# Experts' second product: 256 row gathers and strip matmuls in place of a dense product with gates

## The chip, the cores and the metric

The kernel runs on one core of a Trainium2 chip. Its time is the device time of one launch in microseconds (us). Three runs of the kernel before gave 1656.79, 1662.8 and 1663.07 us; the median is 1662.8. The core has five instruction queues that matter here: TensorE (PE, with the weight loads shown apart as PEld), VectorE (DVE), ScalarE (ACT), GpSimd (POOL) and SyncE (SP), which issues the loads. Sixteen DMA engines move the data.

## The reference, cut to what matters

The program is three residual layers with their feed-forwards and mixers on 256 tokens of 1,024 channels in float32, and at the end a layer of 16,384 experts, `peer`. Only that last layer is touched.

```python
def peer(h, w_query, sub_keys1, sub_keys2, expert_u, expert_v):     # T = 256 tokens, D = 1024
    q = (hf @ w_query).reshape(T, PEER_HEADS, 2, PEER_QDIM // 2)    # 8 heads
    s1 = jnp.einsum('thc,hkc->thk', q[:, :, 0], sub_keys1)          # 128 first keys
    s2 = jnp.einsum('thc,hkc->thk', q[:, :, 1], sub_keys2)          # 128 second keys
    v1, i1 = lax.top_k(s1, PEER_TOPK)                               # 16 of each
    v2, i2 = lax.top_k(s2, PEER_TOPK)
    cand = (v1[..., :, None] + v2[..., None, :]).reshape(T, PEER_HEADS, PEER_TOPK * PEER_TOPK)
    vc, ic = lax.top_k(cand, PEER_TOPK)
    idx = (e1 * N_KEYS + e2).reshape(T, PEER_HEADS * PEER_TOPK)     # 128 experts per token
    gate = jax.nn.softmax(vc, axis=-1).reshape(T, PEER_HEADS * PEER_TOPK)
    def block(args):                                                # per 128 tokens
        u = expert_u[ib]
        pre = jnp.einsum('td,tkd->tk', xb, u)
        a = jax.nn.gelu(pre, approximate=False) * gb
        return jnp.einsum('tk,tkd->td', a, expert_v[ib])            # the second product
    ...
```

Every token picks 128 of the 16,384 experts. Expert tables `expert_u` and `expert_v` hold 16,384 rows of 1,024 floats each, 64 MB a table.

## The kernel before

The layers ahead of the experts are the same in both kernels and end near 790 us of the span. What follows runs in three stages.

**Queries and scores.** Sixteen steps `q_step` and `s_step`: a unit of 128 x 1,024 weights comes in on SP's queue, ScalarE rounds it to a high part (`whi`, L70), VectorE takes the rest as a low part (`wlo`, L73), and TensorE multiplies high by high, low by high and high by low (`mm_ws`, L351): 24 matmuls of 256 columns. The picks are found by VectorE (`top16`: maxima, their places, their removal) in a background list `bg` from which `run_bg` hands out as much as a step's allowance permits. GpSimd adds the candidates and masks the places; it also makes `dg_p`, from which TensorE spreads the norm's token factors (`rows_of`, L342).

**Up-products.** 128 steps `u_step`, one for each first key `e`: the 128 experts (e, 0..127) against all 256 tokens, 24 matmuls, so the first product is dense: it is made for all experts, picked or not. The result of the Gelu goes to `GS[e // 64][:, e % 64]`, a store of 128 second keys x 128 first keys x 256 tokens. Before them the tokens are normalised in place (`norm_a`, `norm_b`, `norm_c`).

**Gates.** The routing weights are put onto the stored activations by one-hot products (`gate_a`, `gate_mm` L1741, `gate_mul`): 32 steps for each half of `GS`, each of eight tokens and 24 small bfloat16 matmuls. The first half's steps are spread over the last fifty `u_step`s, the second half's over the first sixty steps of the next stage.

**Second product.** 128 units of `expert_v` come in on SP's queue in order, are split in two parts as the weights are, and twelve matmuls of 512 columns a unit (`mm_xs`, L356 to L358) add onto four banks `acc`: dense again, with zero weight for experts that were not picked. At the end the residual `xd` is added and stored.

The order on TensorE, VectorE and ScalarE is that of the program text (`manual_schedule`); SP and GpSimd take their work as the scheduler puts it. `ahead` starts the load and the split of the next unit one step before it is used; four raw buffers and three of each part form the ring.

Of the kernel before, what the change touches and what calls it, by code (L numbers as in the profile page):

```python
# [46 lines left out]
NW = 232  # L47
# [9 lines left out]
def tile_kernel(ctx: ExitStack, tc: tile.TileContext, x, w, eu, ev, pp, cst, rows, ifb, wif, bias, wqk, subk, out, stage=99, dbg=None):  # L57
# [120 lines left out]
    def rsqrt(y, v, n, nm, pool=wk, e=G):  # L178
        """y = v ** -0.5 on [128, n]: the exponent halved through the bits, three Newton steps."""
# [152 lines left out]
    def rows_of(r, at=None, e=G):  # L332
        """r [128, 2] as rows [128, 256], the same on every partition"""
# [12 lines left out]
    def mm_ws(p, hi, lo, off, kn, rh, rl, stride=128):  # L346
        """p[128, n] = sum_k W[:, k]^T x[:, k]: weights stationary"""
# [6 lines left out]
    def mm_xs(p, xhi, xlo, hi, lo, first, last):  # L354
        """p += x^T W (x stationary), three parts"""
# [4 lines left out]
    def xs_block(n=512, tag="mm", hook=None, ps=None, es=()):  # L360
        """one block of n columns, x stationary: two banks [128 tok, n]; the first two units may be done"""
# [38 lines left out]
    # =====================================================================  # L400
    # layer 0: sliding-window attention with sinks beside the S5 mixer
    # =====================================================================
    def even_layer(_):
# [1627 lines left out]
```

## Time and profile before

| | us |
|---|---|
| median of three runs | 1662.8 |
| lowest and highest run | 1656.79, 1663.07 |
| profiled execution, span from the first to the last instruction | 1656.3 |
| TensorE busy in the span | 1616.3 (98%) |
| VectorE, ScalarE, GpSimd busy | 1182.5, 811.5, 196.0 |
| up-products with half of the gate steps | 840.4 to 1254.3 |
| second product with the other half | 1254.3 to 1652.5 |
| mean of the DMA engines | 162 GB/s |

The page lists no time of the profiled execution other than its span; of the three runs the lowest is 0.5 us above it and the median 6.5. A busy TensorE is not one at its peak, since ends of matmuls are modelled; a matmul in float32 shows as two records where its operands are not of the reduced kind.

### The profile page before, as it was taken

The page shows a single profiled execution, that of the slowest core. Times are in us where ns is not written, and L with a number is a line of the kernel's source. Part 1 is how long each engine was busy: PE and PEld are TensorE (multiplying, and loading weights), DVE is VectorE, ACT ScalarE, POOL GpSimd, SP SyncE. Part 2 cuts the span into 40 slices and gives each one's busy share as a digit, 9 for nine tenths or more (in the row PEclk, how much of TensorE's full clock was granted, in tenths as well). Part 3 has the DMA queues.
Part 4 walks back from the last instruction along what each step waited for, and adds up shares of the span by engine and source line. Part 5 has one row for each costly group of instructions (what it writes and reads, how often), then busy time and mean ns, then how long its engine had stood idle before and what let it go on. Part 6 is the DMA issues. An engine that isn't in the chain of part 4 may idle for free.

```text
span 1656.3 us, 29543 instructions
## 1 busy us (share of the span) xinstructions
PE 1616.3 (98%) x11722; PEld 1460.5 (88%) x11722; DVE 1182.5 (71%) x2138; ACT 811.5 (49%) x1367; POOL 196.0 (12%) x345
## 2 busy tenths in 40 slices
PE   5899999999999999999999999999999999999999
PEld 4769999989899998777999999999998888888887
DVE  8787766655666667756799898677777888865555
ACT  4447444557754445476654545433334333344453
POOL 6931100011100000401110324000000000000000
PEclk9969999999999999999999999999999999999999
DMA  5415655553445565534555556544444444456664
GB/s 175 112 38 172 215 186 184 186 173 115 141 153 185 184 190 168 185 112 142 186 171 190 173 189 196 174 136 130 138 132 149 152 150 144 144 180 196 193 191 165
DMA packets 77970, 268.93 MB, mean 162 GB/s; under 512 B 9856, under 2 KB 13060, under 8 KB 77576
## 3 DMA queue, kind: packets, MB, share of 16 engines
q1 hardware_dynamic: 76776, 266.27, 50.4%
q8 instruction: 91, 1.49, 0.4%
q10 hardware_dynamic: 1056, 0.79, 0.2%
q14 instruction: 47, 0.39, 0.1%
HBM read 264.40 MB, written 2.62 MB: 161 GB/s over the span
## 4 chain that ended last, share of the span: by engine, by line
PE 89%; DVE 5%; POOL 3%; ACT 1%; issue 1%; DMA 1%; SPq 0%; POOLq 0%; ACTq 0%; DVEq 0%
PE mm L351 40%; PE acc L356 11%; PE acc L357 11%; PE acc L358 11%; PE mm L1741 3%; PE acc L1741 3%; DVE wlo L73 1%; PE acc L235 1%; POOL cmG L73 1%; PE acc L690 1%; PE mm L766 1%; PE mm L356 1%; PE mm L358 1%; PE mm L357 1%; PE mm L193 0%
## 5 line engine op out<-in xcount | busy, mean ns | idle before, releaser
L73 DVE TENSOR_TENSOR wlo<-raw,whi 128x1024 fp32r<-128x1024 f32 x473 | 588.6, 1246 | 280.9 <-ACT whi L70 271.7
L70 ACT ACTIVATE whi<-raw 128x1024 fp32r<-128x1024 f32 x475 | 502.3, 1058 | 439.2 <-PE acc L357 235.2
L351 PE MATMUL mm<-xh,whi 128*128 128x256 f32 x1472 | 212.3, 287 | 0.0
L351 PE MATMUL mm<-xh,wlo 128*128 128x256 f32 x1472 | 206.8, 283 | 0.0
L351 PE MATMUL mm<-xl,whi 128*128 128x256 f32 x1472 | 206.4, 283 | 0.0
L356 PE MATMUL acc<-whi,vh 128*128 128x512 f32 x512 | 202.1, 395 | 0.0
L357 PE MATMUL acc<-whi,vl 128*128 128x512 f32 x512 | 199.5, 390 | 0.0
L358 PE MATMUL acc<-wlo,vh 128*128 128x512 f32 x512 | 199.3, 389 | 0.0
L351 PEld LDWEIGHTS mm<-xh,whi 128*128 128x128 f32 x1472 | 193.0, 192 | 4.4
L351 PEld LDWEIGHTS mm<-xl,whi 128*128 128x128 f32 x1472 | 189.9, 192 | 0.0
L351 PEld LDWEIGHTS mm<-xh,wlo 128*128 128x128 f32 x1472 | 189.7, 192 | 0.0
L67 ACT ACTIVATE gs<-mm 128x256 f32<-128x256 f32 x128 | 49.2, 385 | 235.5 <-PE mm L351 235.4
L358 PEld LDWEIGHTS acc<-wlo,vh 128*128 128x128 f32 x512 | 96.1, 188 | 20.3
L356 PEld LDWEIGHTS acc<-whi,vh 128*128 128x128 f32 x512 | 96.8, 189 | 19.0
L357 PEld LDWEIGHTS acc<-whi,vl 128*128 128x128 f32 x512 | 96.2, 188 | 19.0
L1741 PEld LDWEIGHTS <-gb 128*128 128x128 bf16 x1536 | 93.5, 118 | 9.3 <-issue 7.8
L73 DVE TENSOR_TENSOR ga<-ga,pkT 128x512 bf16<-128x512 bf16 x192 | 75.4, 421 | 2.2
L351 PE MATMUL mm<-nh,wlo 128*128 128x256 f32 x512 | 70.8, 280 | 0.1
L351 PE MATMUL mm<-nh,whi 128*128 128x256 f32 x512 | 70.2, 279 | 0.0
L351 PE MATMUL mm<-nl,whi 128*128 128x256 f32 x512 | 70.1, 279 | 0.0
L357 PE MATMUL acc<-whi,fhl 128*128 128x512 f32 x176 | 69.6, 395 | 0.4 <-DVE fhl L73 0.4
L356 PE MATMUL acc<-whi,fhh 128*128 128x512 f32 x176 | 69.3, 399 | 0.0
(530 smaller groups left out, 2377.6 us busy)
## 6 DMA issues: line engine op xcount, KB each, us to landing
raw<-in_w_dram SPq DMA_DIRECT2D x232, 512.0 KB, 3.5
raw<-in_eu_dram SPq DMA_DIRECT2D x128, 512.0 KB, 3.7
raw<-in_ev_dram SPq DMA_DIRECT2D x128, 512.0 KB, 3.5
x<-in_x_dram SPq DMA_DIRECT2D x2, 512.0 KB, 5.7
bias_t<-in_bias_dram SPq DMA_DIRECT2D x1, 1024.0 KB, 7.2
xd<-x SPq DMA_DIRECT2D x2, 512.0 KB, 3.1
subk_t<-in_subk_dram SPq DMA_DIRECT2D x1, 1024.0 KB
xr<-xd SPq DMA_DIRECT2D x2, 512.0 KB, 3.2
```

The lines of the kernel that those rows point to most:

```text
L67: return A.activation(o, i, f, **k)
L70: return A.activation(o, i, AF.Copy)
L73: return (e or V).tensor_tensor(o, a, b, op=op)
L235: T.matmul(ps[u][:, 0:256], nx[u][l][:, k * 128:(k + 1) * 128], x_[:, k], start=part == 0 and k == 0, stop=part == 2 and k == 7)
L351: T.matmul(p, l[:, off + k * stride:off + k * stride + 128], r[:, k, :], start=(a == 0 and k == 0), stop=(a == 2 and k == kn - 1))
L356: T.matmul(p, xhi, hi, start=first, stop=False)
L357: T.matmul(p, xlo, hi, start=False, stop=False)
L358: T.matmul(p, xhi, lo, start=False, stop=last)
L690: T.matmul(o, qT[rr, per * b + i, js], kT[rr, :n], start=i == 0, stop=False, skip_group_check=True)
L766: T.matmul(sp[half][i][:, s8 * 64:(s8 + 1) * 64], bct[i][half][:, s8], u4[:, half * 8 + s8, LC - 1], start=True, stop=True)
L1741: T.matmul(p[:, i * EB:(i + 1) * EB], o[:, i // 4, :, i % 4], a[:, k, i // 4, :, i % 4], start=k == 0, stop=k == 2)
```

## The change

The up-products stay dense, but nothing is normalised ahead of them and their raw results are kept: `GS` is now one store for all 128 first keys, the scores, the sub-keys and the tables of the picks lie in its last rows until the up-products overwrite them, and ScalarE copies instead of applying the Gelu. The gate steps and the dense second product are gone.

In their place stand 64 slots `s` of four tokens, one token from each quarter of a 128-token tile (`tok`):

- `gather`: four indirect DMAs from GpSimd's queue, each fetching the 128 picked rows of `expert_v` of one token (128 x 4 KB) by the row numbers in `pidx`, into fourteen buffers that the ring and the two copies of x held before (`slot`); three slots ahead.
- `spread`: four small bfloat16 matmuls put the second keys of each token's picks on all partitions; VectorE compares them with the partition number, which gives one-hot columns.
- `extract`: four float32 matmuls of those columns with the token's 128 x 128 block of `GS`, read in steps of 256 elements; VectorE picks the first key's entry by a compare-and-sum, then come the norm factor, the Gelu, the routing weight, and a 128 x 32 tile `w32` per token with the weights in column `s % 32`.
- `apply`: eight float32 matmuls with 32 weight columns and 512 moving columns; the four tokens write to the four strips of 32 partitions of a bank, and 32 slots accumulate into it.

`store` adds the residual after slots 31 and 63. GpSimd's queue now follows the program text as well.

```diff
@@ peer layer: store and tables
-    GS[0] = p2.tile([128, EB, 256], F32, name="gs0", tag="gs0")
...
+    GS = p2.tile([128, 128, 256], F32, name="gs")
+    scs = GS[:, 112:128].rearrange("p e t -> p (e t)")
+    subk_t = GS[:, 104:112].rearrange("p e t -> p (e t)").rearrange("p (m k) -> p m k", m=16)
...
+    G.memset(eye, 0.0)
+    G.memset(eye.rearrange("p a b -> p (a b)")[:, 0:1024:33], 1.0)
...
+        V.tensor_copy(pe1[:, js], p[:, 0:128])
+        stt(pidx[:, js], pe1[:, js], 128.0, p[:, 128:256], OP.mult, OP.add)
+        V.tensor_copy(pg[:, js], p[:, 256:384])
...
     def u_step(e):
...
-        mm_ws(p[:, :256], hi, lo, 0, 8, *((nh, nl) if e < EB else (xh, xl)))
-        act(GS[e // EB][:, e % EB], p[:, :256], AF.Gelu)
+        mm_ws(p[:, :256], hi, lo, 0, 8, xh, xl)
+        cp(GS[:, e], p[:, :256])
...
-    def gate_mm(a, o, pool):
-        p = bank(*pool)
-        for i in range(8):
-            for k in range(3):
-                T.matmul(p[:, i * EB:(i + 1) * EB], o[:, i // 4, :, i % 4], a[:, k, i // 4, :, i % 4], start=k == 0, stop=k == 2)
-        return p
...
+    kinds = ["raw"] * 4 + ["whi"] * 3 + ["wlo"] * 3 + ["xh"] * 2 + ["xl"] * 2
...
+    def gather(s):
+        out_ = []
+        for g in range(4):
+            v = slot()
+            G.indirect_dma_start(v, None, evr, bass.IndirectOffsetOnAxis(ap=pidx[:, tok(s, g):tok(s, g) + 1], axis=0))
+            out_.append(v)
+        return out_
...
+    def spread(s):
+        p = bank()
+        for g in range(4):
+            c = tok(s, g) % 128
+            T.matmul(p[:, g * 128:(g + 1) * 128], idb[:, c:c + 1].to_broadcast([128, 128]), e2b[:, s // 32],
+                     start=g == 0, stop=True, skip_group_check=True)
+        o = p2.tile([128, 512], F32, name="o2", tag="o2", bufs=3)
+        ts(o, p, pcol[:, 0:1], None, OP.is_equal)
+        xs_[s] = o
+
+    def extract(s):
+        o = xs_.pop(s)
+        p = bank()
+        for g in range(4):
+            T.matmul(p[:, g * 128:(g + 1) * 128], o[:, g * 128:(g + 1) * 128], GS[:, :, tok(s, g)],
+                     start=g == 0, stop=True, skip_group_check=True)
+        pk = p2.tile([128, 4], F32, name="pk", tag="pk", bufs=2)
+        for g in range(4):
+            t = tok(s, g)
+            stt(jk, iota, pe1[:, t:t + 1], p[:, g * 128:(g + 1) * 128], OP.is_equal, OP.mult, accum_out=pk[:, g:g + 1])
+        mul(pk, pk, toks(rb_p, s))
+        act(pk, pk, AF.Gelu)
+        mul(pk, pk, toks(pg, s))
+        w32 = p2.tile([128, 4, 32], F32, name="w32", tag="w32", bufs=3)
+        mul(w32, pk[:, :, None].to_broadcast([128, 4, 32]), eye[:, s % 32, None, :].to_broadcast([128, 4, 32]))
+        return w32
+
+    def apply(s, vs, w32):
+        j, i = s // 32, s % 32
+        for hf in range(2):
+            for g in range(4):
+                T.matmul(acc[j][hf][32 * g:32 * g + 32], w32[:, g], vs[g][:, hf * 512:(hf + 1) * 512],
+                         start=i == 0, stop=i == 31, skip_group_check=True)
...
@@ the last loop
-        for e in range(128):
-            hi, lo = VW.next()
-            ahead()
-            if e < 126:
-                v_split(e + 2)
...
-                    mm_xs(acc[j][hf], ah[:, sl], al[:, sl], hi[:, c], lo[:, c], e == 0, e == 127)
...
-            gates[1].until((e + 1) / 60)
...
+        vs = [gather(s) for s in range(3)]
+        spread(0)
+        spread(1)
+        ws_ = [extract(0)]
+        for s in range(NS):
+            if s + 2 < NS:
+                spread(s + 2)
+            if s + 1 < NS:
+                ws_.append(extract(s + 1))
+            apply(s, vs.pop(0), ws_.pop(0))
+            if s + 3 < NS:
+                vs.append(gather(s + 3))
+            if s == 31:
+                store(0)
+        store(1)
```

On TensorE's queue before, this is the end of one unit of the second product and the beginning of a gate step (`whi`, `wlo` the parts of the expert rows, `vh`, `vl` those of the stored activations, `ga`, `gb` the one-hot factors):

```order
L356 MATMUL acc<-whi,vh 128x512
L357 MATMUL acc<-whi,vl 128x512
L358 MATMUL acc<-wlo,vh 128x512
L1741 LDWEIGHTS gb [waits DVE_49]
L1741 MATMUL mm<-ga,gb 128x64 [waits DVE_49]
L1741 LDWEIGHTS gb
L1741 MATMUL mm<-ga,gb 128x64 [waits DVE_49]
```

The unit's twelve matmuls wait for no load by name, since the parts were made a step early; a gate step waits for VectorE.

On the same queue now, this is the end of a `spread` (L1753), an `extract` (L1764) and an `apply` (L1781) of the main loop (`vt`, `vx` are the gathered rows, DMASW0 to DMASW7 the eight semaphores of the gathers, `o` the one-hot columns, `w` the weights):

```order
L1753 LDWEIGHTS idb
L1753 MATMUL mm<-e2b,idb 128x128
L1764 MATMUL mm<-gs,o_13803 128x128 [waits DVE_49]
L1764 MATMUL mm<-gs,o_13803 128x128 x3
L1781 MATMUL acc<-vt,w_13818 32x512 [waits DMASW0_49,DVE_49]
L1781 MATMUL acc<-vt,w_13818 32x512 [waits DMASW1_49]
L1781 MATMUL acc<-vx,w_13818 32x512 [waits DMASW2_49]
L1781 MATMUL acc<-vx,w_13818 32x512 [waits DMASW3_49]
L1781 MATMUL acc<-vt,w_13818 32x512 x2
L1781 MATMUL acc<-vx,w_13818 32x512 x2
```

Each of the first four applies now waits for a gather of its own, and with the first one everything that TensorE has behind it; the spread and the extract of later slots stand in front.

On GpSimd's queue before, at the start of the query stage (`one_p` and `dg_p` serve the spread of the token factors, `cand` the picks, `xh`, `xl`, `nh`, `nl` the copies of x):

```order
L1586 MEMSET one_p 128x128 [waits DMAHW4_49,DMAHW5_49,DMAHW3_49,DMAHW6_49,DMAHW2_49,DMAHW7_49,DVE_49,PE_49]
L86 TENSOR_SCALAR dg_p<-c_76,rc 128x128 [waits Pool_49]
L86 TENSOR_SCALAR dg_p<-c_76,rc 128x128
L73 TENSOR_TENSOR cand<-tv 128x256 [waits DMAHW7_49,DMAHW0_49,DVE_49]
L73 TENSOR_TENSOR cand<-tv 128x256 [waits DVE_49]
L1820 COPY xh<-nh 128x256 [waits PE_49,Activation_49] x5
L1821 COPY xl<-nl 128x256 [waits PE_49] x5
```

The fill of `one_p` and the two halves of `dg_p` follow one another.

On the same queue now, at the same place:

```order
L1582 MEMSET one_p 128x128 [waits DMAHW3_49,DMAHW4_49,DMAHW2_49,DMAHW5_49,DMAHW0_49,DMAHW6_49,DVE_49,DMAHW7_49,PE_49,Pool_49]
L1592 MEMSET eye 128x1024
L86 TENSOR_SCALAR dg_p<-c_76,rc 128x128
L1593 MEMSET eye 128x32 [waits Pool_49]
L86 TENSOR_SCALAR dg_p<-c_76,rc 128x128
L73 TENSOR_TENSOR cand<-gs 128x256 [waits DVE_49] x2
L73 TENSOR_TENSOR cand<-gs 128x256 [waits DVE_49,Pool_49] x6
```

A fill of 1,024 columns stands between `one_p` and `dg_p` now, and the copies of x are gone; the work on the picks comes next.

GpSimd's queue before ends with the last masks of the picks (`toh`). Now the gathers follow them (`pidx` the row numbers):

```order
L73 TENSOR_TENSOR toh<-toh,gs 128x256 [waits DVE_49,Pool_49] x16
L1742 DMA vt<-in_ev_dram,pidx 128x1024 [waits DMAHW4_49,DMAHW1_49,DMAHW5_49,DMAHW0_49,DVE_49]
L1742 DMA vt<-in_ev_dram,pidx 128x1024 [waits DMAHW5_49,DMAHW2_49,DMAHW6_49,DMAHW1_49,DVE_49]
L1742 DMA vt<-in_ev_dram,pidx 128x1024 [waits DMAHW3_49,DMAHW6_49,DMAHW2_49,DVE_49]
L1742 DMA vt<-in_ev_dram,pidx 128x1024 [waits DMAHW7_49,DMAHW3_49,DVE_49]
L1742 DMA vt<-in_ev_dram,pidx 128x1024 [waits PE_49] x3
L1742 DMA vt<-in_ev_dram,pidx 128x1024
L1742 DMA vt<-in_ev_dram,pidx 128x1024 [waits DMASW0_49]
L1742 DMA vt<-in_ev_dram,pidx 128x1024 [waits DMASW1_49]
L1742 DMA vx<-in_ev_dram,pidx 128x1024 [waits DMASW2_49]
L1742 DMA vx<-in_ev_dram,pidx 128x1024 [waits DMASW3_49]
L1742 DMA vx<-in_ev_dram,pidx 128x1024 [waits DMASW4_49]
```

The first four wait for loads and VectorE (the raw buffers), the next for TensorE's last reads of the ring; a later gather waits for the one eight before it by its semaphore and, where the ring comes round, for the apply that frees its buffer.

## Rows read from the trace of the kernel before

**Rows 1.** head of the page: span; busy us, share, instructions by engine

```profile
span 1656.3 us, 29543 instructions
...
PE 1616.3 (98%) x11722; PEld 1460.5 (88%) x11722; DVE 1182.5 (71%) x2138; ACT 811.5 (49%) x1367; POOL 196.0 (12%) x345
```

**Rows 2.** the page's chain that ended last, share of the span by engine

```profile
PE 89%; DVE 5%; POOL 3%; ACT 1%; issue 1%; DMA 1%; SPq 0%; POOLq 0%; ACTq 0%; DVEq 0%
```

**Rows 3.** windows of two stages: us, busy and count by engine, clock, DMA, GB/s

```profile
840.70:1254.30 413.60, 413.50 (x3847) 411.43 (x3846) 337.21 (x735) 178.05 (x265) 46.43 (x55) 1.00 0.52 163
...
1254.30:1650.60 396.30, 396.30 (x2298) 330.42 (x2296) 275.64 (x438) 173.23 (x255) 0.00 (x0) 1.00 0.53 166
```

**Rows 4.** chain by pieces: start us, us, engine, tile, line, matmul records

```profile
828.69 0.44 PE mm L1611 x4
...
1101.23 5.80 PE mm L351 x48
...
1107.03 1.48 PE acc L1741 x24
...
1257.51 0.23 PE acc L357
```

**Rows 5.** line L1741, the gate matmuls: duration ns min/median/max, first and last start

```profile
L1741 PE MATMUL acc<-ga,gb x768: 227/240/246, 1067.5 to 1242.5; 128*128 128x64 bf16 x192
...
L1741 PE MATMUL mm<-ga,gb x768: 226/240/248, 1254.1 to 1464.5; 128*128 128x64 bf16 x192
```

**Rows 6.** tile vh, matmuls of the second product, columns as in rows 5

```profile
L358 PE MATMUL acc<-wlo,vh x512: 388/389/398, 1257.6 to 1652.1; 128*128 128x512 f32 x171
```

**Rows 7.** timeline of POOL, 791 to 800 us: start us, us, instruction

```profile
792.22 0.19 POOL L73 TENSOR_TENSOR nr<-nr,nu 128x2 f32<-128x2 f32 x1
...
795.00 0.46 POOL L1586 MEMSET one_p<- 128x128 f32 x1
...
795.46 3.11 POOL L86 TENSOR_SCALAR dg_p<-c,rc 128x128 f32<-128x128 f32 x2
```

**Rows 8.** costliest groups of the page: the gate steps' weight loads

```profile
L1741 PEld LDWEIGHTS <-gb 128*128 128x128 bf16 x1536 | 93.5, 118 | 9.3 <-issue 7.8
```

**Rows 9.** timeline of PE: eight 32-column float32 matmuls in four strips, twice

```profile
91.18 1.94 PE L838 MATMUL mm<-u,kt 128*32 128x256 f32 x16
...
108.88 1.07 PE L838 MATMUL mm<-u,kt 128*32 128x256 f32 x16
```

**Rows 10.** windows around these, columns as in rows 3

```profile
91.10:93.10 2.00, 2.00 (x18) 0.65 (x17) 1.97 (x4) 1.62 (x6) 0.02 (x1) 0.50 0.00 0
...
108.80:110.00 1.20, 1.20 (x20) 0.54 (x20) 0.66 (x1) 1.20 (x3) 0.00 (x0) 1.00 0.00 0
```

**Rows 11.** groups by form, DVE and ACT: count, busy us, mean ns, idle before

```profile
L703 DVE TENSOR_REDUCE mx<-acc 128x2 f32<-128x512 f32 x4 | 2.6, 681 | 0.9 <-PE acc L691 0.9
...
L90 DVE SCALAR_TENSOR_TENSOR asc<-acc,bias_t 128x128 f32<-128x128 f32 x8 | 1.8, 281 | 0.0
...
L73 DVE TENSOR_TENSOR hdn<-hdn,col 128x4 f32<-128x4 f32 x2 | 0.3, 163 | 1.4 <-ACT hdn L67 1.4
...
L67 ACT ACTIVATE hdn<-ht 128x4 f32<-128x4 f32 x2 | 0.4, 209 | 0.0
```

**Rows 12.** windows where the DMA engines were full, columns as in rows 3

```profile
9.70:12.70 3.00, 0.23 (x2) 0.00 (x0) 2.73 (x10) 0.67 (x1) 1.80 (x4) 1.00 1.05 414
...
669.70:672.70 3.00, 3.00 (x15) 2.49 (x14) 0.00 (x0) 0.94 (x1) 0.00 (x0) 1.00 1.03 419
...
668.70:673.70 5.00, 5.00 (x24) 4.12 (x23) 1.33 (x2) 1.94 (x3) 0.54 (x1) 1.00 0.92 370
```

**Rows 13.** the page's DMA queue of the loads, and expert loads to landing

```profile
q1 hardware_dynamic: 76776, 266.27, 50.4%
...
raw<-in_ev_dram SPq DMA_DIRECT2D x128, 512.0 KB, 3.5
```

**Rows 14.** groups by form, POOL, the same shape as dg_p at another place

```profile
L86 POOL TENSOR_SCALAR ndg<-c,nr 128x128 f32<-128x128 f32 x4 | 2.7, 674 | 0.2
```

More of the change, by code (lines that the diff above doesn't have):

```diff
@@ new lines, in tile_kernel, with tk_tile @@
+    e2b = p2.tile([128, 2, 128], BF16, name="e2b")
+    idb = p2.tile([128, 128], BF16, name="idb")
+    V.tensor_copy(idb, ident)
+    pcol = p2.tile([128, 1], F32, name="pcol")
+    eye = p2.tile([128, 32, 32], BF16, name="eye")
+    G.memset(eye, 0.0)
+    G.memset(eye.rearrange("p a b -> p (a b)")[:, 0:1024:33], 1.0)
+    tk = GS[:, 96:104].rearrange("p e t -> p (e t)")
+    tk_at = [0]
+    def tk_tile(n, *shape, dt=F32):
+        t = tk[:, tk_at[0]:tk_at[0] + n]
+        tk_at[0] += n
+        if dt is not F32:
+            t = t.bitcast(dt)
+        names = "abcd"[:len(shape)]
+        return t.rearrange("p (%s) -> p %s" % (" ".join(names), " ".join(names)), **dict(zip(names, shape)))
@@ L1671, in top_c @@
         st_j[j]["gt"] = gt
-        st_j[j]["e12"] = p2.tile([128, 2, 8, 16], F32, name="e12", tag="e12", bufs=1)
+        st_j[j]["e12"] = te12
         st_j[j]["qf"] = []
@@ new lines, in u_step, with slot @@
+        cp(GS[:, e], p[:, :256])
+    NS = 64
+    slots = []
+    evr = ev.rearrange("a b d -> (a b) d")
+    tok = lambda s, g: 128 * (s // 32) + 32 * g + s % 32
+    toks = lambda t, s: t[:, 128 * (s // 32) + s % 32:128 * (s // 32) + s % 32 + 97:32]
+    kinds = ["raw"] * 4 + ["whi"] * 3 + ["wlo"] * 3 + ["xh"] * 2 + ["xl"] * 2
+    n_slot = [0]
+    half_ = [None]
+    def slot():
+        k = kinds[n_slot[0] % len(kinds)]
+        first = n_slot[0] % 2 == 0
+        n_slot[0] += 1
+        if k in ("xh", "xl"):
+            if first:
+                half_[0] = acts.tile([128, 2, 1024], F32, name="vx", tag=k)
+            return half_[0][:, 0 if first else 1]
+        return ring.tile([128, 1024], F32, name="vt", tag=k, bufs=4 if k == "raw" else 3)
@@ new lines, in apply, with store @@
+    def apply(s, vs, w32):
[4 more added lines that the diff above has]
+                         start=i == 0, stop=i == 31, skip_group_check=True)
+    def store(j):
+        for hf in range(2):
+            c = slice(hf * 512, (hf + 1) * 512)
+            xr = p2.tile([128, 512], F32, name="xr", tag="o2", bufs=3)
+            S.dma_start(xr, xd[j * 128:(j + 1) * 128, c])
+            add(xr, xr, acc[j][hf])
+            S.dma_start(out[j * 128:(j + 1) * 128, c], xr)
@@ L1788, in tile_kernel @@
     UW = Stream(eu, ring, 4, "u", 3)
-    VW = Stream(ev, ring, 4, "u", 3)
     def ahead():
-        for st_, n_ in ((W, NW), (UW, 128), (VW, 128)):
+        for st_, n_ in ((W, NW), (UW, 128)):
             if st_.i < n_:
@@ L1795, in ahead @@
                 return
-    vh = [None, None]
-    def v_split(e):
-        if e == 0:
-            vh[:] = [acts.tile([128, 8, 256], F32R, name=n_, tag=t_) for n_, t_ in (("vh", "xh"), ("vl", "xl"))]
-        split(vh[0][:, e % 8], vh[1][:, e % 8], GS[e // EB][:, e % EB])
-    with tc.manual_schedule(engines={mybir.EngineType.PE, mybir.EngineType.DVE, mybir.EngineType.Activation}):
+    with tc.manual_schedule(engines={mybir.EngineType.PE, mybir.EngineType.DVE, mybir.EngineType.Activation, mybir.EngineType.Pool}):
         qs = [q_step(m) for m in range(3)]
@@ L1813, in tile_kernel @@
                 top_a(m - 1)
-            for k, f_ in ((m - 5, norm_c), (m - 4, norm_b), (m - 3, norm_a)):
-                if 0 <= k < 8:
-                    f_(k)
-            run_bg(0.8)
+            run_bg(1.2)
         top_a(15)
-        for k in range(8):
-            G.tensor_copy(xh[:, k], nh[:, k])
-            G.tensor_copy(xl[:, k], nl[:, k])
-        gates = [Gates(0, ("acc", 4)), Gates(1, ("mm", 4))]
         u = [0]
```

128 lines of the change are left out of this document (20 added, 108 removed).

## The prediction

> **What bounds the kernel now.** I read the head of the page first. The reader is to see that TensorE is busy for 98% of the span of 1656.3 us and that GpSimd is nearly idle, at 12% [rows 1]. The chain that ended last says the same about time: 89% of it is TensorE, DMA is 1% [rows 2]. So in the last third, which the change replaces, time is what TensorE has to multiply. The windows by stage bear this out: in the expert up-products (840.7 to 1254.3) and in the second product (from 1254.3) TensorE is busy without a gap at a granted clock of 1.00, that is 2.4 GHz, while the DMA engines are half idle and GpSimd does nothing in the second product [rows 3]. The chain, piece by piece, gives the unit prices: 48 up-product matmuls, two units, take 5.80 us, one gate step of 24 small matmuls 1.48 us, one matmul of the second product 0.23 us [rows 4].
>
> **What goes.** The 128 units of the second product with 12 matmuls each are gone, and so are all 64 gate steps. Half of the gate steps stand in the up-product stage (768 matmuls, 1067.5 to 1242.5), half in the second product [rows 5]; 32 x 1.48 = 47.4 us come out of the up-products, which then end at 1254.3 - 47.4 = 1206.9. The second product runs from 1254.3 to the end of its last matmul, 1652.1 + 0.4 = 1652.5 [rows 6]; of these 398 us, 32 x 1.48 = 47 are gates and 128 x 12 x 0.23 = 353 the product. Together 446 us of TensorE's time leave the path. What is late next in the up-product stage is again TensorE: VectorE was busy there for 337 of 414 us [rows 3] and loses the gate vectors, the normalised copies go, ScalarE copies where it took the Gelu. I count these at nothing, since TensorE covers them. GpSimd's queue has two fills of "eye" now before dg_p, for which TensorE waits early in the query stage; a fill of 128 x 128 took 0.46 us, so one of 1,024 columns takes up to 3.7, and dg_p's pair was done at 798.6 [rows 7], one unit of 2.9 us before TensorE came to it; the fills cost 0 to 1 us there. I take 0.
>
> **What comes.** 64 slots of four tokens. Each slot takes four gathers, 512 KB apiece: 256 gathers, 134 MB, twice the bytes of the dense product. Three engines work on a slot beside each other.
>
> TensorE: four spreads by weight loads of that shape and type, 4 x 0.118 = 0.47 us [rows 8]; four extracts in float32, by the score products (two such matmuls, four records, 0.44 us [rows 4]) 0.88; eight applies of 32 columns. For these the S5 part has the nearest thing: eight float32 matmuls of 256 columns into the four strips of 32 partitions took 1.07 us at clock 1.00 and 1.94 us at 0.50 [rows 9, 10]. One after the other they would need 8 x 0.44 = 3.5 us, with twice the 0.22 us of a 128-column product each; so the strips do run side by side, and 512 columns give 2 x 1.07 = 2.1 us. Sum 3.5 us per slot. The extract reads its moving operand in steps of 1 KB, which no row shows; if it ran at half rate, 4.4 us.
>
> VectorE: one comparison of 128 x 512 out of PSUM 0.68, four multiply-and-sum of 128 x 128 at 0.28, three small products (0.16, 0.16, 0.28) around a Gelu of 0.2: 2.6 us in a row [rows 11]. The weights of a slot are made one slot early, so this lies beside TensorE's work.
>
> The gathers: the likeliest bound. The DMA engines were full for 3 us at a time in two places, at 414 and 419 GB/s [rows 12]: 512 KB in 1.27 us. A stretch of 5 us around one of them made 370 GB/s, 1.42 us [rows 12]. Below 1.27 us a gather can't go. Above there is no row for an indirect DMA at all: GpSimd issues none before. The far end is one gather at a time, the 3.5 us from issue to landing of a 512 KB unit [rows 13]; but eight semaphores let eight gathers be under way. I take 1.42 us, the nearest row with starts and ends of DMAs in it, and keep 1.27 and 3.5 for the range. Four gathers then take 5.7 us, more than TensorE's 3.5 and VectorE's 2.6, so they set the pace; the first four start before the up-products end, because only the four raw buffers must be free for them, and the rest of the first three slots covers the first weights (about 5 us). So 252 gathers x 1.42 = 357 us, then the last apply 2.1 us, and the same end as before, 1656.3 - 1652.5 = 3.8. The store of the first half at slot 31 holds VectorE for one load of 256 KB, once, some 3 us: within the slot's slack.
>
> The Trainium skill, in "DMA: Bandwidth & Descriptors", section "Anatomy of one DMA — SWDGE (gpsimd) path", gives a DMA from GpSimd 2.0 us plus its bytes over 436 GB/s, which for a gather is an estimate of 3.2 us, and says that the fixed part is mostly waiting for completion. This case's 3.5 us to landing beside 1.27 us of pace agree with a latency that overlaps; if the fixed part did not overlap, 252 x 3.2 would be 806 us.
>
> **Sum.** 1206.9 + 357 + 2.1 + 3.8 = 1570 us of span, 86 less than the 1656.3 of the profiled execution. The runs' median is 1662.8, 6.5 above that span; with the same distance I predict 1576 us. With 1.27 us a gather it is 1539.
>
> **Rivals.**
> 1. GpSimd's own work for a gather sets the pace, slower than the DMA engines. For it: 128 row numbers have to be turned into addresses by an engine that took 0.19 us for two numbers per partition and 1.56 us for 128 x 128, and the same shape cost it 0.67 us elsewhere [rows 7, 14], so it can be slowed to more than twice. Against it: nothing else stands in its queue in that stage. From (1656.3 - 1206.9 - 5.9) / 252 = 1.76 us per gather on the kernel is slower. At 2.2 us, the middle between 1.42 and 3.5 by ratio, 252 x 2.2 = 554 gives a span of 1767, a time of 1774.
> The Trainium skill, "SBUF — State Buffer", section "Summary: rules for kernel authors", warns of just this: a DMA whose descriptors GpSimd writes is starved beside VectorE in its fast modes, and reads by GpSimd wait for VectorE instructions with two SBUF inputs. The 1.56 beside 0.67 us agree in direction; here such VectorE instructions are 0.6 us of a slot, so by the rule up to 64 x 0.6 = 39 us more where GpSimd sets the pace.
> 2. TensorE's clock falls, because it now waits for rows. At a clock of 0.50 around 91 us, where its work was sparse, the eight strip matmuls took 1.94 us [rows 9, 10]; 3.5 us become 6.3, and 64 x 6.3 = 403 us with a start of 5 and the end of 3.8 make 1619, a time of 1625: still faster. Against it: TensorE has work in three fifths of each slot, and a slower clock fills its gaps.
> 3. The bytes eat the gain: rows picked at random move more slowly than units in order. At 1.76 us (298 GB/s) the gain is gone, 1663. The busy share of the load queue over the whole kernel, 266.27 MB in 50.4% of 1656.3 us [rows 13], is 319 GB/s or 1.64 us: 1633.
>
> **Chances.** The forecast (gathers at 1.27 to 1.55 us, 1539 to 1610) 0.48; clock or slower rows, still faster (1610 to 1654), 0.14; within 0.5% 0.05; GpSimd over 1.79 us, slower, 0.33. Half a per cent, 8 us, is about what the spread of the runs (6.3 us) lets one tell from no change. The range: below 1536 I leave 0.03, and above 1790, which is 2.26 us a gather, 0.17; the forecast's own range is 1539 to 1610.
>
> **What would show it.** Right: the up-products end near 1207 without gate matmuls; the DMA busy share after that is 0.85 or more at 360 to 415 GB/s; TensorE is busy for about 60% and waits for gathers; GpSimd's queue waits for a semaphore before each gather. Wrong: DMA share near one half with GpSimd's gathers back to back at over 1.76 us; or a granted clock of 0.5 through the stage; or TensorE records of the applies that follow one another rather than lie beside each other, 7 us a slot by 8 x 4 x 0.22.

## The result, and the profile after

The changed kernel took 1603.2 us (median of 4 runs, 1594.4 to 1607.5) against 1662.9 before: a ratio of 0.9648, 95% interval 0.9613 to 0.9683, or 3.5% faster. The forecast was 1576.

One fact has to be known before any other number is read: measured three more times without a change, on three chips, the same kernel took 1553.4, 1596.6 and 1600.8 us (ratios to the kernel before on the same chip 0.9345 [0.9325, 0.9365], 0.9625 [0.9598, 0.9652] and 0.9655 [0.9635, 0.9676]), and every run of a measurement agreed with the others of it within 0.9%. The kernel before does not tell these chips apart: 1663.0, 1658.9 and 1657.4 us. I call the chip with 1553 kind A and those near 1600 kind B; the first measurement, whose chip is not recorded, is of kind B. Each chip was measured on one occasion only, so a kind is a name for what was seen, and whether it belongs to the chip or to the occasion is not shown. In what follows kernels are compared inside one kind.

The head of the page of after (first measurement, kind B), and the chain that ended last, against [rows 1, 2]:

```profile
span 1599.3 us, 26899 instructions
...
PE 1475.4 (92%) x10442; PEld 1234.1 (77%) x10442; DVE 984.4 (62%) x2240; ACT 643.1 (40%) x1164; POOL 430.6 (27%) x587
...
PE 83%; DVE 7%; POOL 3%; issue 2%; ACT 2%; another core or an unknown queue 1%; DMA 1%; SPq 0%; POOLq 0%; ACTq 0%; DVEq 0%
```

GpSimd's busy share has more than doubled (the gathers), and VectorE's share of the chain has grown from 5% to 7%, but that of DMA is 1% as before: the page does not look like a kernel that waits for its rows.

The chain in order of time (start, us, what), where the last up-product ends and at the end, against [rows 4]:

```profile
842.74 96.03 PE mm L351 x800
...
1212.34 0.25 PE mm L1753 x4
...
1583.08 1.10 issue
1584.18 2.03 PE mm L1764 x8
...
1588.78 6.57 PE acc L1781 x32
...
1595.37 0.69 DVE xr L73
```

The up-products end at 1212.3 without gates, the last product at 1595.4. In between lie 383 us for 64 slots, 6.0 us each. The windows of this kernel (us, busy and count of PE, PEld, DVE, ACT, POOL, then clock, DMA share, GB/s), against [rows 3]:

```profile
840.00:1212.00 372.00, 371.96 (x3101) 371.76 (x3101) 244.13 (x503) 172.53 (x265) 49.29 (x52) 1.00 0.58 182
...
1300.00:1350.00 50.00, 39.58 (x236) 19.41 (x233) 22.80 (x98) 1.64 (x8) 31.06 (x34) 0.82 0.97 351
...
1400.00:1450.00 50.00, 39.22 (x240) 18.47 (x232) 24.75 (x109) 1.85 (x9) 31.65 (x34) 0.84 0.99 371
```

The DMA engines are marked busy at 0.97, TensorE has idle time, and its granted clock has a mean of 0.82. On kind A the same program reads otherwise. Its windows, and the end of its chain:

```profile
1300.00:1350.00 50.00, 48.79 (x275) 22.32 (x278) 27.44 (x118) 1.85 (x9) 34.65 (x37) 1.00 1.03 408
1400.00:1450.00 50.00, 48.78 (x271) 22.23 (x270) 26.29 (x112) 1.85 (x9) 35.65 (x39) 1.00 1.03 409
```

```profile
1535.70 10.09 DMA vt<-in_ev_dram,pidx
1545.80 0.04 issue
1545.84 1.92 PE acc L1781 x10
```

Here the clock stays at 2.4 GHz, 408 GB/s pass, 512 KB every 1.285 us, and the chain ends in the landing of the last gather. So there are two things to explain: what sets the pace on kind A, and what takes another 45 us on kind B.

The durations of the new instructions on kind A (ns, min/median/max; first and last start), by their lines: gather, spread, extract, apply.

```profile
L1742 POOL DMA_INDIRECT vt<-in_ev_dram,pidx x183: 932/936/947, 1200.4 to 1535.7; - x183
```

```profile
L1753 PE MATMUL mm<-e2b,idb x256: 217/219/235, 1211.8 to 1531.2; 128*128 128x128 bf16 x128
```

```profile
L1764 PE MATMUL mm<-gs,o x512: 393/395/464, 1213.1 to 1538.4; 128*128 128x128 f32 x171
```

```profile
L1781 PE MATMUL acc<-vt,w x736: 589/592/617, 1217.7 to 1547.2; 128*32 128x512 f32 x184
```

A gather holds GpSimd for 0.94 us and is followed by 0.30 us at least before the next: 1.24 us. That is 0.04 us below the pace of the transfers, so two engines stand almost level.

Now a slot of kind B. From its timeline (start, us, engine, line; in brackets the idle time before and who ended it), TensorE and VectorE from 1335 to 1346 us of after (L1753 spread, L86 comparison, L1764 extract, L90 multiply-and-sum, L1781 apply):

```profile
1335.47 0.40 PE L1753 MATMUL mm<-e2b,idb 128*128 128x128 bf16 x4
...
1335.70 1.95 PE L1764 MATMUL mm<-gs,o 128*128 128x128 f32 x8
...
1337.58 1.92 PE L1781 MATMUL acc<-vx,w 128*32 128x512 f32 x16
...
1340.18 0.75 DVE L86 TENSOR_SCALAR o<-mm,pcol 128x512 f32<-128x512 f32 x1 [3.89 <-PE mm L1753]
...
1340.98 1.99 PE L1764 MATMUL mm<-gs,o 128*128 128x128 f32 x8 [1.15 <-DVE o L86]
...
1343.04 0.35 DVE L90 SCALAR_TENSOR_TENSOR jk<-c,pe,mm 128x128 f32<-128x128 f32 x1 [2.11 <-PE mm L1764]
...
1345.65 1.93 PE L1781 MATMUL acc<-vt,w 128*32 128x512 f32 x8 [2.67 <-DVE w L73]
```

The comparison at 1340.18 reads the spread that was over at 1335.87, and VectorE had been free since 1336.28: it starts 3.9 us late. The multiply-and-sum at 1343.04 reads the extract that was over at 1337.65 (the engines keep the written order, comparison and then multiply, and counting slots from the start of the stage pairs them so). On kind A the same two follow 0.03 to 0.05 us behind the end of the product they read, here a comparison behind its spread:

```profile
1300.08 0.40 PE L1753 MATMUL mm<-e2b,idb 128*128 128x128 bf16 x4
...
1300.52 0.75 DVE L86 TENSOR_SCALAR o<-mm,pcol 128x512 f32<-128x512 f32 x1 [0.85 <-PE mm L1753]
```

On kind B TensorE then waits for the weights. In such pauses its granted clock falls to 0.50, that is 1.2 GHz, at which the apply that follows takes 3.64 us in place of 1.92. One of them, a window of 2 us in the pause and the apply behind it:

```profile
1308.00:1310.00 2.00, 0.24 (x4) 0.20 (x8) 1.62 (x8) 0.20 (x1) 1.39 (x3) 0.50 1.02 408
...
1309.76 3.64 PE L1781 MATMUL acc<-vt,w 128*32 128x512 f32 x16 [2.66 <-DVE w L73]
```

### The profile page after: what moved, and what is told of

Read it like the earlier page. It is cut to its first block, busy times and chain, and to the rows that moved or that the text cites. A ratio compares the mean times of both kernels' runs of the same rounds, so it can differ in the third digit from the quotient of the medians.

```text
span 1599.3 us, 26899 instructions
## 1 busy us (share of the span) xinstructions
PE 1475.4 (92%) x10442; PEld 1234.1 (77%) x10442; DVE 984.4 (62%) x2240; ACT 643.1 (40%) x1164; POOL 430.6 (27%) x587
## 4 chain that ended last, share of the span: by engine, by line
PE 83%; DVE 7%; POOL 3%; issue 2%; ACT 2%; another core or an unknown queue 1%; DMA 1%; SPq 0%; POOLq 0%; ACTq 0%; DVEq 0%
PE mm L351 43%; PE acc L1781 9%; PE mm L1764 7%; PE acc L357 4%; PE acc L356 4%; PE acc L358 4%; DVE jk L90 2%; PE mm L1753 2%; POOL cmG L73 1%; PE acc L235 1%; PE acc L690 1%; DVE wlo L73 1%; DVE o L86 1%; PE mm L766 1%
## 5 line engine op out<-in xcount | busy, mean ns | idle before, releaser
L73 DVE TENSOR_TENSOR wlo<-raw,whi 128x1024 fp32r<-128x1024 f32 x345 | 426.3, 1237 | 251.7 <-ACT whi L70 239.8
L70 ACT ACTIVATE whi<-raw 128x1024 fp32r<-128x1024 f32 x347 | 365.9, 1056 | 221.7 <-issue 97.9
L351 PE MATMUL mm<-xh,wlo 128*128 128x256 f32 x1984 | 279.4, 284 | 0.0
L351 PE MATMUL mm<-xl,whi 128*128 128x256 f32 x1984 | 279.1, 283 | 0.0
L1742 POOL DMA_INDIRECT vt<-in_ev_dram,pidx x184 | 173.2, 941 | 287.3 <-DVE wlo L73 186.6
L1781 PE MATMUL acc<-vt,w 128*32 128x512 f32 x736 | 133.7, 719 | 33.5 <-DVE w L73 31.7
L1764 PE MATMUL mm<-gs,o 128*128 128x128 f32 x512 | 127.7, 403 | 24.0 <-DVE o L86 14.6
L90 DVE SCALAR_TENSOR_TENSOR jk<-c,pe,mm 128x128 f32<-128x128 f32 x256 | 88.8, 347 | 76.2 <-PE mm L1764 56.7
L1764 PEld LDWEIGHTS mm<-gs,o 128*128 128x128 f32 x512 | 101.2, 220 | 32.7 <-DVE o L86 16.2
L86 DVE TENSOR_SCALAR o<-mm,pcol 128x512 f32<-128x512 f32 x64 | 47.8, 748 | 107.1 <-PE mm L1753 56.5
L1781 PEld LDWEIGHTS acc<-vt,w 128*32 128x32 f32 x736 | 25.7, 122 | 88.4 <-issue 48.5
L1781 PE MATMUL acc<-vx,w 128*32 128x512 f32 x288 | 71.1, 804 | 24.2 <-DVE w L73 24.2
```

The costliest lines, as they stand in the source:

```text
L70: return A.activation(o, i, AF.Copy)
L73: return (e or V).tensor_tensor(o, a, b, op=op)
L86: return (e or V).tensor_scalar(o, a, s1, None, op0=op0)
L90: return V.scalar_tensor_tensor(o, a, s, b, op0=op0, op1=op1, **k)
L351: T.matmul(p, l[:, off + k * stride:off + k * stride + 128], r[:, k, :], start=(a == 0 and k == 0), stop=(a == 2 and k == kn - 1))
L1742: G.indirect_dma_start(v, None, evr, bass.IndirectOffsetOnAxis(ap=pidx[:, tok(s, g):tok(s, g) + 1], axis=0))
```

## The experiments

Theories of the first round: the bytes through the DMA engines set the pace (1); GpSimd's work for a gather (2); TensorE and VectorE (3); the random order of the rows (4). The four kernels e1, e2, e3 and e6 ran on one chip before the two kinds were known. The unaltered kernel was not measured on that chip. I count it as kind A, because the four show what kind A shows: a granted clock of 1.00 from 1300 us on, landing times in the trace and, in e2 and e3, 409 GB/s. So their measure is the 1553.4 us of e0_after_again, from another chip, and not the 1603 named in the expectations; the effects expected are read as differences.

**e1_half_rows.** Half a row (2 KB) is fetched for each number, and both halves of the product read it.

```diff
-    evr = ev.rearrange("a b d -> (a b) d")
+    evr = ev.rearrange("a b (h d) -> (a b h) d", h=2)
...
-            G.indirect_dma_start(v, None, evr, ...)
+            G.indirect_dma_start(v[:, 0:512], None, evr, ...)
...
-   ... vs[g][:, hf * 512:(hf + 1) * 512],
+   ... vs[g][:, 0:512],
```

> The gathers fetch half rows (2 KB instead of 4 KB a row, 256 KB a gather, the table read as 32768 half rows) and both halves of the product use the same half; every instruction of TensorE, VectorE and GpSimd stays. After: 1603 us, 1.49 us a gather through the stage. Theory 1 (the bytes through the DMA engines set the pace): the engines' part falls to about 0.75 us a gather, and the next bound takes over, GpSimd's own 0.94 us an instruction with 0.30 us between, 1.24 us, or TensorE at about 1.2 to 1.3 us a gather: about 250 x 0.22 = 55 us less, 1535 to 1560. Theory 2 (GpSimd's making of the descriptors sets the pace): no change, 1603 within 6. Theory 3 (the spread, extract and apply of TensorE at its half clock free the buffers too late and set the pace): no change, 1603 within 6.

Measured: 1537.8 us, ratio 0.9266 [0.9227, 0.9305], 15.6 less than the kernel on kind A, not the 50 that the bytes alone would give. Its window and its gathers:

```profile
1300.00:1350.00 50.00, 48.56 (x277) 22.72 (x280) 27.20 (x117) 2.05 (x10) 38.03 (x40) 1.00 0.72 210
```

```profile
L1742 POOL DMA_INDIRECT vt<-in_ev_dram,pidx x184: 942/947/1175, 1200.0 to 1527.0; - x184
```

DMA is no bound any more at a share of 0.72; the pace is 512/2 KB at 210 GB/s, 1.25 us a gather, which is GpSimd's 0.947 + 0.30. A gather lands 3.8 us after its issue at the median, 9.5 in the unaltered kernel. So on kind A theory 1 holds down to 1.25 us, and there theory 2 takes over.

**e2_rows_in_order.** A gather reads 128 rows that lie side by side.

```diff
-        stt(pidx[:, js], pe1[:, js], 128.0, p[:, 128:256], OP.mult, OP.add)
+        ts(jk, iota, 128.0, pcol[:, 0:1], OP.mult, OP.add)
+        V.tensor_copy(pidx[:, js], jk)
```

> The list of rows is replaced by rows in order (partition p of a token reads row 128 x token + p, modulo 16384), so that a gather reads 512 KB side by side; everything else stays. After: 1603 us, 1.49 us a gather. Theory 1 (the engines move 4 KB packets at their rate wherever they come from): 1603 within 6. Theory 4 (rows in random order cost the memory time): the pace falls to the 1.27 us of full streaming (414 GB/s), 250 x 0.2 = 50 us less, 1550 to 1560, or to GpSimd's 1.24 us.

Measured: 1554.2 us, 0.9363 [0.9326, 0.9399], the same as unaltered on kind A (0.9345). The order of the rows costs nothing there. On kind B it was not tried.

**e3_no_extract.** No spread and extract after the first slot.

```diff
-        spread(1)
...
-            if s + 2 < NS:
-                spread(s + 2)
-            if s + 1 < NS:
-                ws_.append(extract(s + 1))
-            apply(s, vs.pop(0), ws_.pop(0))
+            apply(s, vs.pop(0), ws_[0])
```

> The loop leaves out the spread and the extract of every slot but the first (8 of a slot's 24 products, VectorE's, ScalarE's small operations); every slot's product takes the weights of slot 0. The gathers and the 16 weight loads and products of a slot stay. Theory 1 (the DMA engines set the pace): 1.43 to 1.49 us a gather, 1590 to 1603; only the last slot's end may shorten. Theory 3 (TensorE and VectorE set it): TensorE's slot falls from about 4.0 us at full clock and up to 7 us at half clock to 1.9 and 3.6 us, and the pace to the next bound, GpSimd's 1.24 us or the engines' 1.43: 1540 to 1590. A time under 1585 says that the extract was on the path.

Measured: 1550.1 us, 0.9336 [0.9300, 0.9373], no difference from unaltered on kind A that the intervals show. My line that under 1585 the extract was on the path was written against the wrong measure and falls. TensorE's waits in its stage (us, times, longest):

```profile
PE acc L1781 <- DMA vt<-in_ev_dram,pidx: 33.4, 131, 1.3
PE acc L1781 <- DMA vx<-in_ev_dram,pidx: 12.8, 53, 0.6
```

With half of its work gone TensorE waits for rows and the pace stays at 409 GB/s: theory 3 is out on kind A. (In the traces the stage is 331 us long here and 336 unaltered.)

**e6_pool_extra.** One fill behind each gather.

```diff
...
+            G.memset(pjunk, 0.0)
```

> One memset of 128x128 on GpSimd is added behind every gather (0.20 us for such a tile in the trace of after, 0.46 in that of before). Theory 2 (GpSimd sets the pace): 256 x 0.2 to 0.46 = 51 to 118 us more, 1654 to 1720. Theory 1 (the DMA engines): GpSimd's 1.24 us back to back becomes 1.44 to 1.70 against 1.49: nothing more with a memset of 0.2 us (1603 within 8), up to 50 us with one of 0.46.

Measured: 1565.7 us, 0.9425 [0.9385, 0.9464], 12.3 us more than unaltered on kind A. The two lines on GpSimd:

```profile
L1743 POOL DMA_INDIRECT vt<-in_ev_dram,pidx x184: 942/944/1179, 1204.1 to 1553.7; - x184
```

```profile
L1744 POOL MEMSET pjunk<- x256: 218/219/231, 1205.3 to 1554.6; 128x128 f32 x128
```

The fill takes 0.22 us, but the idle time between a fill and the next gather is 0.17 us, so a gather costs GpSimd 0.94 + 0.22 + 0.17 = 1.33. Against the transfers' 1.285 that is 256 x 0.045, some 12 us. The whole 12.3 does not lie there: in its profiled run, the slowest of the four, the up-products end 6.5 us later than in e0_after_again (1218.3 and 1211.8), and the gather stage is 345 us long against 336, 9 us more. A gather lands after 6.3 us at the median, 9.5 unaltered, so fewer of them lie over each other: GpSimd has just become the bound. GpSimd's price of a plain gather is the 1.25 us of e1.

**e0_after_again, e7_two_ahead, e5_runs_of_8** ran on one chip. All kernels of the first round had kept the full clock; theory 5 was that the program falls into the bunched order of the timeline above, and theory 6 concerned the stride of the extract. e0_after_again has no edit. e7 makes the weights one slot earlier (with a fourth w32 buffer):

```diff
...
-            if s + 2 < NS:
-                spread(s + 2)
-            if s + 1 < NS:
-                ws_.append(extract(s + 1))
+            if s + 3 < NS:
+                spread(s + 3)
+            if s + 2 < NS:
+                ws_.append(extract(s + 2))
```

and e5 stores the dot products in runs of eight (the other views of this memory are left out):

```diff
-    GS = p2.tile([128, 128, 256], F32, name="gs")
+    GS = p2.tile([128, 16, 256, 8], F32, name="gs")
...
-        cp(GS[:, e], p[:, :256])
+        cp(GS[:, e // 8, :, e % 8], p[:, :256])
```

> The changed kernel itself, unaltered, beside the next two on one chip. The four kernels of the first round all ran TensorE at full clock through the gather stage and moved 380 to 410 GB/s where full rows were fetched; the changed kernel had run at a mean granted clock of 0.83 there and 350 GB/s. Theory 5 (the changed program itself falls into a bunched rhythm, in which VectorE and TensorE wait for each other, TensorE pauses, its clock falls and gathers start late): again 1594 to 1608 with a stage clock near 0.83. Rival (that one chip or run was slow): 1555 to 1570, as the kernel with the extra memset.

> The spread and the extract of a slot's weights are done one slot earlier (spread three, extract two slots ahead of the product, w32 with four buffers); nothing else changes. Theory 5 (bunched rhythm: the product waits for VectorE's weights, 121 us of TensorE's idle time in the changed kernel, since they are made one slot ahead only): the waits on w go, the clock stays at 1.00, the pace falls to 1.27 to 1.33 us a gather: 1550 to 1570. Rival (GpSimd's bursts of gathers at 1.24 us slow the packets, and the memset helped by spacing them): no change, 1595 to 1608.

> The table of dot products is laid out so that the extract's moving operand reads runs of 8 elements (32 bytes) instead of single ones 1 KB apart; ScalarE's copy into the table writes elements 32 bytes apart instead of a run. Theory 6 (the stride doubles the extract's duration): the 8 products of a slot fall from 1.78 us to 0.9 to 1.0, TensorE's slot from about 4.0 to 3.2 us. Theory 1 (DMA bound): the time does not follow, 1595 to 1608, unless the shorter slot also ends the bunched rhythm, then 1550 to 1570. ScalarE's copies, 128 of 0.38 us, may grow; they lie beside TensorE's 2.9 us a group.

Measured: 1553.4 (0.9345), 1557.1 (0.9372 [0.9348, 0.9397]) and 1558.0 us (0.9376 [0.9354, 0.9399]): no difference that these intervals show. The unaltered kernel was itself at the lower value, so for e7 and for the second half of e5's question nothing follows. What e5 does show is the price of the stride (extract of e5, then ScalarE's copies in its up-products; kind A unaltered had 395, and the copies took 384 ns in after):

```profile
L1764 PE MATMUL mm<-gs,o x512: 275/275/377, 1213.7 to 1538.1; 128*128 128x128 f32 x171
```

```profile
L70 ACT ACTIVATE gs<-mm 128x256 f32<-128x256 f32 x128 | 84.4, 659 | 174.4 <-PE mm L351 174.4
```

A record of the extract falls from 395 to 275 ns with runs of 32 bytes, the copies rise from 384 to 659, beside TensorE. The eight records of a slot go from 1.95 to 1.11 us. The time does not follow, as theory 1 says.

**e0b_after_third, e9_one_stall, e10_more_traffic** ran on another chip, which was of kind B. e0b has no edit; e9 stalls VectorE once; e10 adds transfers of which nothing is used, on SyncE's queue (the spare tiles are left out).

```diff
...
+            if s == 8:
+                for _ in range(30):
+                    V.memset(vjunk, 0.0)
```

```diff
...
+            if s > 1:
+                act(tiny[:, 0:1], djunk[s % 2][:, 0:1], AF.Copy)
+            S.dma_start(djunk[s % 2], ev[s][:, 0:256])
+            S.dma_start(ejunk[s % 2], ev[s][0:32])
```

> The changed kernel unaltered for a third measurement, in five rounds. It was 1603 us in the first measurement (1594 to 1607, clock 0.83 and 350 GB/s in the stage) and 1553 in the second (clock 1.00, 408 GB/s). Theory 7 (the slow first measurement came from outside the program): 1553 to 1560 again, or now and then near 1600, but a whole measurement at one of the two. Theory 5 (the program has two rhythms and falls into one or the other by chance in each run): the runs of this measurement are mixed, some near 1553, some near 1600.

> Once, behind the product of slot 8, VectorE gets 30 memsets of 128x512 (9 to 15 us in all), so that the weights of the next slots come late and TensorE pauses; nothing else changes. Theory 5 (once out of step, the loop stays in the bunched rhythm with the clock falling at every pause): the stage stays at 1.45 to 1.5 us a gather to its end, 1590 to 1610. Theory 7 (the rhythm does not hold itself): the clock falls once, the buffers are refilled within some slots, and the pace is 1.27 us again: 1553 plus at most the stall, 1555 to 1568.

> Each slot moves 256 KB more on SyncE's queue (128 KB from DRAM into a spare tile in 1 KB rows, 128 KB from DRAM to DRAM), 12.5% of the slot's 2 MB; the results are not used. Theory 1 (the DMA engines' bytes set the pace): 5.1 us a slot becomes 5.7 to 6.0 us: 1590 to 1610. On the first measurement: if slower transfers alone make the bunched rhythm, the clock of the stage falls to 0.8 to 0.9 and VectorE waits for TensorE's signals as there; if not, the clock stays at 1.00 with TensorE waiting for the gathers alone, at the same 5.7 to 6.0 us a slot.

Measured: 1596.6, 1609.4 (0.9699 [0.9667, 0.9731]) and 1603.5 us (0.9650 [0.9619, 0.9680]). All six runs of e0b lie between 1593 and 1605, so the two times belong to the measurement, not to the single run: theory 7. The stall of e9, 19.6 us long, shows in its windows; the first line is a window of its control, e0b:

```profile
1300.00:1350.00 50.00, 38.10 (x228) 18.86 (x224) 22.49 (x97) 1.65 (x8) 32.41 (x35) 0.80 0.97 355
...
1212.00:1260.00 48.00, 38.33 (x234) 20.50 (x233) 22.69 (x97) 3.31 (x10) 30.14 (x33) 0.89 0.94 339
1260.00:1300.00 40.00, 21.01 (x132) 9.93 (x130) 27.09 (x86) 0.82 (x4) 17.68 (x19) 0.74 0.68 254
1300.00:1350.00 50.00, 40.76 (x255) 20.21 (x252) 22.45 (x101) 1.85 (x9) 32.51 (x36) 0.86 0.97 357
```

It costs 12.8 us and leaves the pace of kind B as it was; as its control was slow already, it can't say whether a stall would have tipped kind A. e10 says more. With 12.5% more bytes its stage moves more in the same time:

```profile
1300.00:1350.00 50.00, 38.81 (x230) 19.09 (x229) 23.06 (x98) 2.39 (x16) 31.17 (x34) 0.86 0.99 380
1350.00:1400.00 50.00, 38.84 (x236) 18.89 (x238) 22.96 (x101) 2.38 (x16) 31.88 (x35) 0.82 1.00 378
```

If the engines' bytes set the pace, 12.5% of its control's stage, 47 of 375 us, would come on top; it was 6.9, and only 4 of these lie in the stage (379 us). That 1603.5 falls into the 1590 to 1610 expected for theory 1 says nothing, as those were reckoned from 1553. So on kind B a DMA share of 0.97 at 355 GB/s is not a full DMA system: theory 1 does not hold there. It does not follow that the gathers themselves could go faster, since the added rows lie in order, come over another queue, and half of them go from DRAM to DRAM.

**e0c_after_fourth, e11_far_ahead** ran on one more chip, again of kind B. Theory 8: the late signals between TensorE and VectorE set the pace there. e11 gives each of them two slots of slack (and o2 and w32 a fourth buffer).

```diff
...
-            if s + 2 < NS:
-                spread(s + 2)
-            if s + 1 < NS:
-                ws_.append(extract(s + 1))
+            if s + 5 < NS:
+                spread(s + 5)
+            if s + 3 < NS:
+                ws_.append(extract(s + 3))
```

> The changed kernel unaltered, as the measure for the next one on the same chip. So far it was 1603, 1553 and 1597 us in three measurements, each of one kind throughout. Theory 7 (the kind belongs to the measurement, that is to the chip it ran on): all runs near 1553 or all between 1593 and 1608.

> The spread runs five and the extract three slots ahead of the product (two and one before), with a fourth o2 and a fourth w32 buffer, so that a signal between TensorE and VectorE may come two slots (10 us) late without a wait; nothing else changes. In the slow kind VectorE starts 2 to 7 us behind the end of the product it reads. Theory 8 (in the slow kind the late signals between TensorE and VectorE set the pace, not the DMA engines, which moved 12.5% more for 7 us): if the control is of the slow kind, 1555 to 1575 here. Theory 1 (there the transfers themselves are slow): no change, 1593 to 1608. If the control is of the fast kind both theories say 1550 to 1560, and the run tells nothing of them.

Measured: 1600.8 (0.9655 [0.9635, 0.9676]) and 1594.3 us (0.9613 [0.9597, 0.9630]). The intervals do not meet, so e11 is faster than the changed kernel on this chip, by 6.5 us; theory 8 wanted 25 to 45. (On the chip before, also of kind B, the unaltered kernel had 1596.6.) What TensorE waits for in the stage, after first, then e11:

```profile
PE acc L1781 <- DVE w L73: 55.9, 22, 3.9
PE mm L1764 <- DVE o L86: 14.6, 11, 4.1
PE mm L1764 <- issue: 9.4, 8, 4.2
```

```profile
PE mm L1764 <- issue: 29.9, 54, 1.4
PE acc L1781 <- issue: 12.3, 20, 1.1
```

The waits for VectorE, 70 us, are gone as intended, and the clock is up, first a window of the control e0c, then two of e11:

```profile
1300.00:1350.00 50.00, 39.90 (x248) 19.72 (x240) 22.24 (x99) 1.64 (x8) 31.36 (x34) 0.88 0.97 354
...
1300.00:1350.00 50.00, 42.27 (x235) 20.28 (x238) 23.45 (x105) 1.77 (x9) 31.45 (x34) 0.91 0.96 355
1350.00:1400.00 50.00, 43.59 (x252) 20.45 (x248) 24.58 (x110) 1.92 (x10) 32.20 (x35) 0.96 0.97 354
```

In their place stand pauses of up to 1.4 us before extracts, some of them inside a run that waits for nothing in the program, and 354 GB/s as before. So the late signals do not set the pace.

Where the time of kind B goes can be read on GpSimd. Its 250 gathers of the stage hold it for 235 us on kind B (after) and 234 on kind A. Its idle time before them is 139 us in after, 140 in e0c and 139 in e11, against 92 in e0_after_again: the 47 us between the kinds are the 383 against 336 us of their stages. On kind B they are pauses of about 2 us. The largest groups behind the regular 0.30 us, after first, then kind A, then e11 (us, times, longest):

```profile
POOL vt L1742 <- PE mm L1764: 24.0, 19, 2.2
POOL vt L1742 <- remote: 16.3, 9, 2.6
```

```profile
POOL vt L1742 <- PE acc L1781: 10.1, 29, 0.4
POOL vt L1742 <- DMA vt<-in_ev_dram,pidx: 6.4, 16, 1.3
```

```profile
POOL vt L1742 <- remote: 38.2, 23, 2.2
```

What ends these pauses the traces cannot tell: in all six profiles of kind B there are no landing times of the gathers, which those of kind A have (9.5 us at the median, unaltered), so the releasers named there are what is left. In GpSimd's queue a gather waits for the one eight before it. So one rival stays untested: that gathers land later there, after some 12 us (8 under way x 1.49 us, an estimate), which the extra bytes of e10 need not change. No run altered the number under way. Another is that the engines themselves pause, as TensorE does inside the extracts of e11. Whether these chips, something else that used them, or the recording on them is at fault was not tried, and I leave it open.

## Why the prediction was right or wrong

**The sum.** The forecast was right in sign and within 1.7% of the first measurement, but between the two kinds rather than on either: 1570 us of span were forecast, 1599.3 and 1551.7 came. Term by term:

- The gates taken out of the up-products: these ran 413.6 us before [rows 3] and 842.7 to 1212.3 = 369.6 after, so 44.0 went of the 47.4 forecast. The stage also began 2.0 us later: ScalarE's first copy of queries now stands 4.4 us, until GpSimd's factor rc is there, where it stood 1.3 us for TensorE before (read from the trace, the reason not tried; VectorE's 3.1 us for rc were there before too). Together the up-products ended 5.4 us late. GpSimd's two fills of "eye" took 0.95 and 0.25 us and held nobody up that the trace shows, as said.
- The gather stage, 357 + 2.1 = 359 us forecast: 383 on kind B, 336 on kind A (1211.8 to 1547.8). This is the term that was mis-sized, by "I take 1.42 us, the nearest row with starts and ends of DMAs in it". On kind A nothing starts and ends: seven to eight gathers lie over each other (9.5 us to landing) and the pace is 1.285 us, near the 1.27 that I had given as the floor [rows 12]. On kind B 1.42 was near the measured 1.49 (249 gathers issued from 1212.6 to 1583.8), but that is luck: a mean of full transfers and their ends is not what happens there. GpSimd issues at 1.24 us and loses the rest in pauses of about 2 us, whose cause is open.
- The end: 3.8 us forecast, 3.9 measured on both. Outside the span 1.7 us lie in the profiled run, not 6.5, which was the distance of a median of runs whose lowest lay 0.5 us above the span.

**TensorE's slot.** The spread took 0.40 us (0.47 forecast), the apply 1.92 (2.1): its strips do run side by side [rows 9]. The extract took 1.95 us, more than twice the 0.88; the case named for it, half rate for steps of 1 KB, is what happened, 4.3 us a slot against the 4.4 given. On kind A it cost nothing, as e3 shows. That TensorE would be busy 60% was wrong in part for the same reason: by the records it was 78% of the stage on kind B and 97% on kind A, where waits for rows count in too (e3, with half of the work, still shows 85%). And what it waited for on kind B was VectorE's weights, not gathers as forecast.

**VectorE's slot** was 3.2 us, not 2.6: between 1302.30 and 1304.79 of kind A the multiply-and-sums come every 0.39 us with a read of the accumulator behind each, and the comparison took 0.75. Made one slot early it hides on kind A; on kind B it does not.

**Rival 1, GpSimd** (0.33): the mechanism is real, its price of 2.2 us was not; 1.24 to 1.25 us is 3% below the transfers' pace, so e1 and e6 both make GpSimd the bound. The Trainium skill's warning on starved descriptors ("SBUF — State Buffer", "Summary: rules for kernel authors") is not borne out by any run here: with VectorE busy for 46% of the stage (after) a gather held GpSimd for 0.94 us at the median and 1.04 at most, and with VectorE all but idle (e3) the median is 0.94 too; whether VectorE was in its fast modes the traces do not say. The fixed 2 us of the Trainium skill's "DMA: Bandwidth & Descriptors" ("Anatomy of one DMA — SWDGE (gpsimd) path") do overlap on kind A: 9.5 us to landing beside 1.285 us of pace.

**Rival 2, the clock** (with rival 3, 0.14): on kind B the clock is at 0.50 after pauses of 2 to 3 us and back at 1.00 later, mean 0.82 (1300 to 1350 us); at 6.0 us a slot that looks like the rival's 6.3. But e11 lifts it to 0.93 over the stage (0.85 in its control) with the gathers still at 354 to 355 GB/s, so it is not the bound. On kind A, unaltered, it was 1.00 through the stage.

**Rival 3, rows in random order:** no cost on kind A (e2); on kind B, at 350 to 360 GB/s, the order of the rows was not varied.

## What to carry to other kernels

Price a gather by the engine that issues it as well as by its bytes: here 1.24 us of GpSimd for 128 rows of 4 KB, 1.25 for rows of 2 KB, against 1.285 us for moving 4 KB rows, so shorter rows gain almost nothing on kind A (half of the bytes saved 1%). Where transfers had no gap between them (kind A), their pace was that of the best full window, not of a window with an end in it. And measure an unaltered kernel again beside the experiments: without the second measurement the first round would have "shown" that four unrelated edits each save 38 to 65 us.

## What was not expected of the hardware

- One program ran at 1553 us on one chip and near 1600 on two others, where the kernel before differed by 0.3%; the difference lies in the stage of the gathers (336 us against 375 to 384 in the profiles of the unaltered kernel; 408 against 350 to 360 GB/s in most windows).
- A DMA share of 0.97 was no proof of a full DMA system: 12.5% more bytes, over another queue, fitted in for 0.4% of the time (e10).
- float32 products that read their moving operand in steps of 1 KB took 395 ns a record, in runs of 32 bytes 275 (e5).
- A GpSimd instruction put between two gathers shortened the idle time before the next gather from 0.30 to 0.17 us (e6).
